# Gathering the experts' tokens in plain float32, two experts at a time, with two more weight blocks in the ring

## The chip, the cores and the metric

The kernel runs on one core of a Trainium2 chip. TensorE multiplies matrices into PSUM (eight banks of 128 x 512 float32 here); VectorE, ScalarE and GpSimd work on SBUF, and the first two also read PSUM; SyncE (SP) issues nearly all DMA transfers that bring weights from HBM. The metric is the device time of one execution in microseconds; a kernel's time is the median of several runs.

## What is computed

The program is two transformer blocks one after the other on 256 tokens of width 1024. The first is a token mixer (attention, gated linear attention, a long convolution), followed by a mixture of experts; the second has two layers, each with attention, a convolutional feed-forward part and a gated projection. Only the mixture of experts, near the middle, is touched. It adds to the residual stream `x`:

```
h = modulate(rms_norm(x, norm2_g), shift2, scale2)
x = x + gate2[:, None, :] * grouped_moe(h, router_w, router_b,
                                        moe_w_gate, moe_w_up, moe_w_down)
```

For every token the router scores 16 experts in 4 groups, keeps the best group and in it the best two experts, and weights them. An expert e computes `(silu(h Wg[e]) * (h Wu[e])) Wd[e]` with Wg and Wu of 1024 x 512 and Wd of 512 x 1024, in float32.

## The kernel before

All instructions are unrolled and their order on each engine is the order in which the Python code emits them (`manual_schedule`). Every operation on TensorE, ScalarE and VectorE goes through the helper `Clocked` (line 379 in the profile's rows), so the rows are told apart by the names of their tiles.

**Precision.** A weight that is used with full precision elsewhere is split into two rounded halves of the type float32r (`T2`, `split`, `mm3`), and three products of halves replace one. Experts use plain float32 matmuls (type F32 on both sides). The gather before the change multiplies both float32r halves of the tokens, `h2H` and `h2L`, by a selection matrix.

**Router.** `ev_out` receives the output projection, forms `x1`, and per half of 128 tokens the normed tokens `h` (`h2s[m]`). `normed2` finishes them. `high(m)` rounds them on ScalarE into `h2H`, `low(m, n)` forms the rest `h2L` on VectorE (for the second half, m = 1, on GpSimd, lines 1591 and 1592). Scores, the two best and their ranks follow on VectorE in instructions of at most 128 x 128 elements (`scores`, `sel`, `ge`, `gt`, `cnt`, `top`, `gs`, `cg`, `mask`); one group of matmuls against `mask` counts, per expert, the tokens ahead. `rank` gives each token its slot in each expert, of 64.

**A branch.** If an expert has more than 64 tokens, a slow body runs (line 1696). It is not taken here, but all engines read the flag from memory and branch. One `gather` ahead of it has its `dp` formed before the branch and its matmuls after it.

**Gather.** `gather(q)` is a Python generator that serves four experts. It forms `dp` (tokens x 4 experts x 64 slots, ones and zeros), then for two quarters of the width multiplies `h2H` and `h2L` (stationary, 128 x 128) by `dp` (moving, 256 columns), 32 matmuls in all, and copies the results into two tiles `xg`. `way(g)` turns `dp` of two experts round (`back`, to send results home) and gathers their gates (`gsl`). A generator runs in steps: at `side.tick()` the planner `Side` runs the next step if the modelled TensorE clock `Clocked.now["P"]` has passed the step's due time, which is the modelled end of what the previous step gave VectorE or ScalarE. For TensorE the model charges columns / 2400 us, four times that for plain float32.

**Experts.** The loop at line 1855 takes one expert after the other. `gate_up(e, i, ps)` uses one 1 MB block of weights: the 64 gathered tokens are stationary, the weights move (512 columns), gate and up in the two column halves of the array. `hidden` turns the result round and forms `hid`; `down(g)` multiplies a pair of experts by the down weights; its result `y` is scaled and split into two halves, and `combine(g - 1)` adds the pair into four PSUM banks `pa` that stay for the whole stage. That leaves four banks for everything else. `gather(1)` is added at expert 1, the next at experts 5 and 9.

**Weights.** The DMA ring holds whole blocks of 1 MB in SBUF slots of 8 KB per partition (`u8`, 19 slots); `load(depth)` issues transfers until `depth` blocks are there or under way, and SP waits in order for each slot. During the experts the depth is `RAW_MOE + 2` = 17; with `h2H` and `h2L` these are the 19 slots. One more block, the 18th, is loaded at line 1627 in two halves into two 4 KB slots (`u4`, 8 slots, which also hold `gate2`, `xg`, `h` and the split `y`).

Of the kernel before, what the change touches and what calls it, by code (L numbers as in the profile page):

```python
# [9 lines left out]
F32 = mybir.dt.float32  # L10
F32R = mybir.dt.float32r
# [7 lines left out]
D = 1024  # L19
# [305 lines left out]
BUFS = {"u8": 19, "u4": 8, "u2": 6, "u1": 4, "uh": 4, "us": 7}  # L325
LAST = 8
RAW = {None: 3, "last": 2, "mod1": 8, "moe_gu": 9, "moe_down": 9}
RAW_MOE = 15
STEPS2 = (1, 1, 1, 0)
STEPS1 = (1, 2, 2, 0, 0, 1, 0, 2)  # L330
PIECES = {"k": 2, "c": 2, "3": 3, "": 1}
# [88 lines left out]
def program(ctx, tc, A, out, dump=None):  # L420
# [80 lines left out]
    def load(depth=None):  # L501
        at = order[pieces[min(pos["take"], len(pieces) - 1)][0]]
        at = "last" if at[0][:8] == "ffn_down" and at[1] >= LAST else at[0]
        while pos["raw"] < len(order):
            i = pos["raw"]
            name, b, kt, cols, _ = order[i]
            if len(raws) >= (depth or (RAW_MOE + 2 if at[:3] == name[:3] == "moe" else RAW.get(at, RAW[None]))):
                break
            if len(raws) >= RAW_MOE + 2:
                raws[i] = [T([128, cols], "raw", tag="u4") for _ in range(kt)]  # L510
                for k, t in enumerate(raws[i]):
                    nc.sync.dma_start(t, A[name][b][:, k * cols:k * cols + cols])
            else:
                t = T([128, kt, cols], "raw", tag="u8")
                nc.sync.dma_start(t.rearrange("p k c -> p (k c)"), A[name][b])
                raws[i] = t if name[:3] != "moe" else [t[:, k] for k in range(kt)]
            pos["raw"] += 1
# [988 lines left out]

    x1 = T([128, 2, D], "x1")

    h2s, rs, h2, turned = {}, {}, [], []

    def ev_out(m, n, ps):

        gate1, shift2, scale2, _ = mod2
        if m and not n:
            turned.extend(turned_half(h2s[0][0], k4) for k4 in range(2))
        c = slice(n * 512, n * 512 + 512)
        if n == 0:
            h2s[m] = T([128, D], "h2"), T([128, 2], "ss2")
        h, ss = h2s[m]
        V.tensor_tensor(x1[:, m, c], ps, gate1[:, c], op=OP.mult)  # L1520
        V.tensor_tensor(x1[:, m, c], x1[:, m, c], xt[:, m, c], op=OP.add)
        j = T([128, 512], "junk2")
        S.activation(j, x1[:, m, c], AF.Square, accum_out=ss[:, n:n + 1])
        V.tensor_tensor(h[:, c], x1[:, m, c], scale2[:, c], op=OP.mult)
        if m and n:
            load(RAW_MOE)
        if not n:
            if m:
                normed2(0)
            return  # L1530
        V.tensor_tensor(ss[:, 0:1], ss[:, 0:1], ss[:, 1:2], op=OP.add)
        rs[m] = rsqrt1(ss[:, 0:1], 1e-6, D)

    def normed2(m, ns=(0, 1)):

        if not m:
            h2.extend(T2([128, 2, D], "h2"))
        h = h2s[m][0] if 0 in ns else h2s[m]
        h2s[m] = h
        for n in ns:  # L1540
            c = slice(n * 512, n * 512 + 512)
            V.scalar_tensor_tensor(h[:, c], h[:, c], rs[m], mod2[1][:, c], op0=OP.mult, op1=OP.add)

    def high(m):
        S.activation(h2[0][:, m], h2s[m], AF.Copy)

    def low(m, n, eng=V):
        c = slice(n * 512, n * 512 + 512)
        eng.tensor_tensor(h2[1][:, m, c], h2s[m][:, c], h2[0][:, m, c], op=OP.subtract)

    pa = [{}, {}]

# [10 lines left out]
    for k4 in range(2):  # L1563
        turned.append(turned_half(h2s[1][0], k4))
        if not k4:
            logits(turned, psr[:, 0:16], True, False)
            residual(0)
    high(0)
    logits(turned[2:], psr[:, 16:32], False, True)
    normed2(1, (0,))  # L1570
    for i in range(1, 3):
        residual(i)
    low(0, 0)
    h2H, h2L = h2
    gate2 = mod2[3]
    dump("x1", x1)

# [8 lines left out]
        V.scalar_tensor_tensor(sg[:, m], psr[:, m * 16:m * 16 + 16], rs[m], st["shifted"], op0=OP.mult, op1=OP.add)  # L1586
    S.activation(sg, sg, AF.Tanh, scale=0.5)
    normed2(1, (1,))
    high(1)
    for n in range(2):  # L1590
        low(1, n, G)
    sel = R(E3, "sel")
    V.scalar_tensor_tensor(sel, sg, 0.5, rb.unsqueeze(1).to_broadcast(E3), op0=OP.mult, op1=OP.add)

    def ahead(v, count):
# [19 lines left out]
    mask = R(E3, "mask")  # L1615
    V.scalar_tensor_tensor(mask.rearrange("p m (g e) -> p (m g) e", e=4), cg2.unsqueeze(2).to_broadcast([128, 8, 4]), 0.5, cnt,
                           op0=OP.is_lt, op1=OP.mult)
    low(0, 1)

    ps = PS()  # L1620
    mf = mask.rearrange("p m e -> p (m e)")
# [14 lines left out]

    grouped = {}

    def gather(q):

        dp = dps[q] = T([128, 2, 4, 64], "dp", F32R)
        shape = [128, 2, 4, 64]
        V.tensor_tensor(dp, rank[:, :, 4 * q:4 * q + 4].unsqueeze(3).to_broadcast(shape),
                        C("slots").unsqueeze(1).unsqueeze(1).to_broadcast(shape), op=OP.is_equal)
        yield
        xg = xgs[q] = [T([128, 4, 4, 64], "xg") for _ in range(2)]
        for k4 in range(2):
            banks = [PS(), PS()]
            for w, src in enumerate((h2H, h2L)):
                for k2, ps in enumerate(banks):  # L1650
                    for m in range(2):
                        for k in range(2):
                            c = slice((k4 * 4 + 2 * k2 + k) * 128, (k4 * 4 + 2 * k2 + k) * 128 + 128)
                            P.matmul(ps[:, k * 256:k * 256 + 256], src[:, m, c], dp[:, m].rearrange("p a s -> p (a s)"),
                                     start=w + m + k == 0, stop=w + m + k == 3)
                if w == 0 and q:
                    yield
            for k2, ps in enumerate(banks):
                p4 = ps.rearrange("p (k a s) -> p k a s", k=2, a=4)
                if k2:  # L1660
                    V.tensor_copy(xg[k4][:, 2:4], p4)
                else:
                    S.activation(xg[k4][:, 0:2], p4, AF.Copy)
            yield

    def way(g):

        d = dps[g // 2][:, :, g % 2 * 2:g % 2 * 2 + 2].rearrange("p m a s -> p m (a s)").bitcast(F32)
        ps = PS()
        for m in range(2):  # L1670
            P.transpose(ps[:, m * 128:m * 128 + 128], d[:, m], ident)
        for a in range(2):
            for m in range(2):
                P.matmul(ps[a * 64:a * 64 + 64, 256:257], d[:, m, a * 64:a * 64 + 64], kept[:, m, 2 * g + a:2 * g + a + 1], start=m == 0, stop=m == 1)
        back, gsl = T([128, 256], "back", F32R), T([128, 1], "gsl")
        S.activation(back, ps[:, :256], AF.Copy)
        V.tensor_copy(gsl, ps[:, 256:257])
        grouped[g] = (back, gsl)

    xgs, dps = {}, {}  # L1680
    first = gather(0)
    next(first)

# [75 lines left out]
    def gate_up(e, i, ps):  # L1759

        w = take("moe_gu", 4 * e + i)
        for k in range(2):
            x = xgs[e // 4][i // 2][:, (2 * i + k) % 4, e % 4]
            for a, q in enumerate((low, high)):
                P.matmul(ps[q], x, w[k][:, a * 512:a * 512 + 512], start=i + k == 0, stop=i + k == 4)
        if i == 3:
            t = T([128, 512], "gu")
            S.activation(t, ps, AF.Copy)
            gated[e] = t
# [13 lines left out]
    def down(g):  # L1783


        back, gsl = grouped.pop(g)
        hid = hids.pop(g)
        ps = [PS(), PS()]
        last = g == N_EXP // 2 - 1
        done[g] = back, []  # L1790
        for i in range(2):
            if not (last and i):
                ws = [take("moe_down", 4 * g + 2 * a + i) for a in range(2)]
            for k, n in ((k, n) for n in range(2) for k in range(2)) if last and i else ((k, n) for k in range(2) for n in range(2)):
                if last and i and not k:
                    wn = take("moe_down", 4 * g + 1 + 2 * n)
                for a, q in enumerate((low, high)):
                    w = wn[a][:, k * 512:k * 512 + 512] if last and i else ws[a][k][:, n * 512:n * 512 + 512]
                    P.matmul(ps[n][q], hid[:, a, 2 * i + k], w, start=i + k == 0, stop=i + k == 2)
                if i and k:  # L1800
                    y = T([128, 512], "y")
                    V.scalar_tensor_tensor(y, ps[n], gsl, gate2[:, n * 512:n * 512 + 512], op0=OP.mult, op1=OP.mult)
                    if not last:
                        hl = T2([128, 512], "y")
                        split(*hl, y)
                    done[g][1].append(y if last else hl)
# [47 lines left out]

    for e in range(N_EXP):
        g = e // 2
        if e % 4 == 1 and e + 3 < N_EXP:
            nxt = side.add(gather(e // 4 + 1))
        ps = PS()
        for i in range(4):  # L1860
            gate_up(e, i, ps)
            if i == 1 and e:
                hidden(e - 1)
            if i == 0 and e % 2:
                way(g)
            if i == 2 and e % 2 and g:
                combine(g - 1)
            if i != 1:
                side.tick()
        if e % 4 == 3 and e + 1 < N_EXP:  # L1870
            side.finish(nxt)
        if e % 2 == 0 and g:
            down(g - 1)
# [490 lines left out]
```

## Time and profile before

| what | value |
|---|---|
| median of 3 runs | 1422.9 us (1419.89 to 1423.99) |
| the profiled execution's own time | 1417.77 us |
| its span from first to last instruction | 1416.0 us |
| mean granted TensorE clock over the span | 0.994 |
| busy: TensorE matmul, weight load, VectorE, ScalarE | 96%, 75%, 59%, 45% |
| weights and other data read from HBM | 295 MB |

The times of the profile are microseconds from the first instruction. PE is TensorE's matmul, PEld its weight load, DVE is VectorE, ACT ScalarE, POOL GpSimd. A row names the tile written, an arrow, and the tiles read, buffer numbers left out. Because matmuls overlap, the ends of matmul rows are modelled; the distance from one start to the next is the better measure of what a group costs. The clock of TensorE is given as a share of 2.4 GHz; 0.50 is its other level, 1.2 GHz.

### The profile page before, as it was taken

What the parts mean: (1) busy time and instruction counts of PE and PEld (TensorE: products, weight loads), DVE (VectorE), ACT (ScalarE), POOL (GpSimd) and SP (SyncE); (2) the same over time, 40 slices, a digit from 0 to 9 for tenths busy, and PEclk for the clock granted to TensorE, in tenths of its full rate; (3) what the DMA queues carried; (4) which work ended last, traced back from release to release, by engine and by line L of the source; (5) the groups of instructions that cost most, each with busy time, mean ns of one, the idle gap of its engine ahead of it and who ended that gap; (6) DMA issues with size and microseconds to landing.
All of it is one profiled execution on the core that took longest, in us unless ns stands there. A gap on an engine that the chain in (4) does not pass through costs nothing.

```text
span 1416.0 us, 20480 instructions
## 1 busy us (share of the span) xinstructions
PE 1365.2 (96%) x8334; PEld 1064.8 (75%) x8334; DVE 836.7 (59%) x1517; ACT 635.8 (45%) x1021; POOL 8.3 (1%) x15
## 2 busy tenths in 40 slices
PE   5999999999999899999999899999999998999998
PEld 2678899878797444343488679999978887999996
DVE  4777457445866511211475586666676888566675
ACT  4643465534433311111356555445536664455541
POOL 0000000000000000000000000000000000000000
PEclk9999999999999999999999999999999999999999
DMA  9523334635469799999742345655544354555630
GB/s 370 223 71 119 149 150 153 250 125 190 175 212 360 301 421 421 421 421 421 283 179 90 120 149 181 207 179 208 175 156 146 127 179 139 188 179 180 216 140 30
DMA packets 44482, 297.42 MB, mean 210 GB/s; under 512 B 5171, under 2 KB 6371, under 8 KB 10017
## 3 DMA queue, kind: packets, MB, share of 16 engines
q1 hardware_dynamic: 41868, 291.02, 54.6%
q10 hardware_dynamic: 1924, 3.27, 0.7%
q0 software_dynamic: 592, 1.79, 0.5%
q8 instruction: 67, 1.10, 0.3%
q14 instruction: 31, 0.25, 0.0%
HBM read 295.00 MB, written 1.05 MB: 209 GB/s over the span
## 4 chain that ended last, share of the span: by engine, by line
PE 58%; DVE 5%; ACT 2%; issue 1%; DVEq 0%; ACTq 0%
PE ps L379 48%; PE pd L379 7%; DVE w L379 1%; PE pa L379 1%; PE pq L379 1%; ACT pe L379 1%; DVE v L379 1%; PE oc L379 1%; DVE sm L379 1%; DVE rs L379 0%; ACT w L379 0%; DVE xL L379 0%; DVE rsa L379 0%; ACT xH L379 0%; ACT oc L379 0%
## 5 line engine op out<-in xcount | busy, mean ns | idle before, releaser
L379 DVE TENSOR_TENSOR w<-raw,w 128x1024 fp32r<-128x1024 f32 (+3 forms) x301 | 346.5, 1195 | 84.6 <-ACT w L379 83.5
L379 ACT ACTIVATE w<-raw 128x1024 fp32r<-128x1024 f32 (+3 forms) x301 | 293.5, 1033 | 10.8 <-DVE w L379 4.8
L379 PE MATMUL ps<-xH,w 128*128 128x256 f32 x1408 | 256.5, 283 | 0.6 <-ACT xH L379 0.6
L379 PEld LDWEIGHTS ps<-xH,w 128*128 128x128 f32 x1408 | 220.6, 192 | 1.8 <-ACT xH L379 1.1
L379 PE MATMUL ps<-xL,w 128*128 128x256 f32 x704 | 199.4, 283 | 0.7 <-DVE xL L379 0.7
L379 PE MATMUL ps<-w,xH 128*128 128x512 f32 (+2 forms) x544 | 150.3, 362 | 4.0 <-ACT xH L379 2.1
L379 PEld LDWEIGHTS ps<-xL,w 128*128 128x128 f32 x704 | 135.0, 192 | 1.8 <-DVE xL L379 1.1
L379 PE MATMUL pd<-w,fh 128*128 128x512 f32 x528 | 125.6, 395 | 0.0
L379 PE MATMUL ps<-raw,xg 128*64 128x512 f32 x512 | 120.0, 600 | 0.0
L379 PE MATMUL ps<-hH,w 128*128 128x256 f32 (+1 forms) x608 | 115.7, 287 | 0.0
L379 PEld LDWEIGHTS pd<-w,fh 128*128 128x128 f32 x528 | 98.2, 189 | 21.6
L379 PEld LDWEIGHTS ps<-w,xH 128*128 128x128 f32 x544 | 95.4, 189 | 19.3 <-ACT xH L379 4.0
L379 PEld LDWEIGHTS ps<-hH,w 128*128 128x128 f32 (+1 forms) x608 | 94.9, 187 | 7.9 <-issue 2.7
L379 PE MATMUL ps<-w,xL 128*128 128x512 f32 (+2 forms) x272 | 97.8, 360 | 1.9 <-DVE xL L379 1.7
L379 PE MATMUL ps<-w,hH 128*128 128x512 f32 (+1 forms) x288 | 88.1, 390 | 0.0
L379 PE MATMUL ps<-hL,w 128*128 128x256 f32 (+1 forms) x304 | 85.9, 283 | 0.0
L379 PEld LDWEIGHTS ps<-raw,xg 128*64 128x64 f32 x512 | 33.3, 137 | 55.7 <-issue 51.9
L379 DVE SCALAR_TENSOR_TENSOR fc<-ps,par,fc 128x255 f32<-128x255 f32 x88 | 42.4, 482 | 51.5 <-ACT fc L379 49.9
L379 ACT ACTIVATE fc<-ps,par 128x256 f32<-128x256 f32 x44 | 24.8, 564 | 92.3 <-PE ps L379 66.4
L379 PEld LDWEIGHTS ps<-w,hH 128*128 128x128 f32 x288 | 52.2, 188 | 13.8 <-issue 2.7
L379 PEld LDWEIGHTS ps<-w,xL 128*128 128x128 f32 x272 | 51.3, 189 | 11.9 <-DVE xL L379 5.1
L379 PE MATMUL ps<-raw,hid 128*64 128x512 f32 x256 | 57.4, 593 | 0.0
(445 smaller groups left out, 1858.7 us busy)
## 6 DMA issues: line engine op xcount, KB each, us to landing
raw<-in_moe_gu SPq DMA_DIRECT2D x63, 1024.0 KB, 14.1
raw<-in_moe_down SPq DMA_DIRECT2D x32, 1024.0 KB, 12.8
raw<-in_mod SPq DMA_DIRECT2D x24, 1024.0 KB, 5.0
raw<-in_ffn_gate SPq DMA_DIRECT2D x22, 1024.0 KB, 4.8
raw<-in_ffn_up SPq DMA_DIRECT2D x22, 1024.0 KB, 4.9
raw<-in_ffn_down SPq DMA_DIRECT2D x22, 1024.0 KB, 4.8
raw<-in_w_brg SPq DMA_DIRECT2D x12, 1024.0 KB, 5.9
raw<-in_ple_gate SPq DMA_DIRECT2D x8, 1024.0 KB, 4.8
```

What stands on the lines that cost most here:

```text
L379: return f(*args, **kw)
```

## The change

The rounded halves `h2H` and `h2L` go, with `high`, `low` and their instructions on ScalarE, VectorE and GpSimd. `gather(g)` now serves two experts: `dp` and `h` are plain float32, a gather is 16 matmuls of 128 columns, and what `way` did is the generator's last step. The gather of the next pair is added at every even expert. The rest of the first gather runs after the second block of expert 0. The two 8 KB slots that the halves held go to the ring: the depth during the experts becomes 19, and line 1627 loads up to 20 blocks; the load in `ev_out` still stops at 15.

```diff
-RAW_MOE = 15
+RAW_MOE = 17
...
         if m and n:
-            load(RAW_MOE)
+            load(RAW_MOE - 2)
...
-        if not m:
-            h2.extend(T2([128, 2, D], "h2"))
...
-    def high(m):
-        S.activation(h2[0][:, m], h2s[m], AF.Copy)
-
-    def low(m, n, eng=V):
-        c = slice(n * 512, n * 512 + 512)
-        eng.tensor_tensor(h2[1][:, m, c], h2s[m][:, c], h2[0][:, m, c], op=OP.subtract)
...
-    high(0)
...
-    low(0, 0)
-    h2H, h2L = h2
...
     normed2(1, (1,))
-    high(1)
-    for n in range(2):
-        low(1, n, G)
...
-    low(0, 1)
...
-    def gather(q):
-
-        dp = dps[q] = T([128, 2, 4, 64], "dp", F32R)
-        shape = [128, 2, 4, 64]
-        V.tensor_tensor(dp, rank[:, :, 4 * q:4 * q + 4].unsqueeze(3).to_broadcast(shape),
+    def gather(g):
+
+        dp = T([128, 2, 2, 64], "dp")
+        shape = [128, 2, 2, 64]
+        V.tensor_tensor(dp, rank[:, :, 2 * g:2 * g + 2].unsqueeze(3).to_broadcast(shape),
                         C("slots").unsqueeze(1).unsqueeze(1).to_broadcast(shape), op=OP.is_equal)
+        d = dp.rearrange("p m a s -> p m (a s)")
         yield
-        xg = xgs[q] = [T([128, 4, 4, 64], "xg") for _ in range(2)]
+        xg = T([128, 8, 2, 64], "xg")
+        grouped[g] = xg,
         for k4 in range(2):
-            banks = [PS(), PS()]
-            for w, src in enumerate((h2H, h2L)):
-                for k2, ps in enumerate(banks):
-                    for m in range(2):
-                        for k in range(2):
-                            c = slice((k4 * 4 + 2 * k2 + k) * 128, (k4 * 4 + 2 * k2 + k) * 128 + 128)
-                            P.matmul(ps[:, k * 256:k * 256 + 256], src[:, m, c], dp[:, m].rearrange("p a s -> p (a s)"),
-                                     start=w + m + k == 0, stop=w + m + k == 3)
-                if w == 0 and q:
-                    yield
...
+            ps = PS()
+            for m in range(2):
+                for k in range(4):
+                    c = slice((k4 * 4 + k) * 128, (k4 * 4 + k) * 128 + 128)
+                    P.matmul(ps[:, k * 128:k * 128 + 128], h2s[m][:, c], d[:, m], start=m + k == 0, stop=m + k == 4)
+            p4 = ps.rearrange("p (k a s) -> p k a s", k=4, a=2)
+            if k4:
+                V.tensor_copy(xg[:, 4:], p4)
+            else:
+                S.activation(xg[:, :4], p4, AF.Copy)
             yield
-
-    def way(g):
-
-        d = dps[g // 2][:, :, g % 2 * 2:g % 2 * 2 + 2].rearrange("p m a s -> p m (a s)").bitcast(F32)
...
-            x = xgs[e // 4][i // 2][:, (2 * i + k) % 4, e % 4]
+            x = grouped[e // 2][0][:, 2 * i + k, e % 2]
...
-        if e % 4 == 1 and e + 3 < N_EXP:
-            nxt = side.add(gather(e // 4 + 1))
+        if e % 2 == 0 and e + 2 < N_EXP:
+            nxt = side.add(gather(g + 1))
...
-            if i == 0 and e % 2:
-                way(g)
+            if e == 0 and i == 1:
+                for _ in first:
+                    pass
...
-        if e % 4 == 3 and e + 1 < N_EXP:
+        if e % 2 and e + 1 < N_EXP:
             side.finish(nxt)
```

## Rows read from the trace of the kernel before

**Rows 1.** Busy time by stretch: length, busy time and count per engine, clock, DMA share, GB/s.
```profile
500.00:685.00 185.00, 185.00 (x923) 73.09 (x921) 30.62 (x56) 26.83 (x53) 0.00 (x0) 1.00 1.01 420
```

**Rows 2.** Chain of waits, 523 to 578 us: start, length, what.
```profile
523.44 22.98 PE ps L379 x114
546.42 2.06 PE pa L379 x8
548.49 27.83 PE ps L379 x146
```

**Rows 3.** Waits of weight loads, 478 to 690 us: total, times, longest.
```profile
PEld ps L379 <- issue: 107.6, 335, 0.8
...
PEld ps L379 <- DMA raw<-in_moe_gu: 0.7, 3, 0.3
```

**Rows 4.** Groups of TensorE instructions by form: busy us, mean ns, idle before.
```profile
L379 PE MATMUL ps<-dp,h2H 128*128 128x256 f32 x64 | 10.3, 308 | 0.3 <-PEq L1696 0.3
...
L379 PE MATMUL oc<-vc,pp 128*128 128x128 f32 x64 | 8.2, 283 | 0.0
```

**Rows 5.** Timeline around one old gather group: start, length, engine, what, count.
```profile
493.28 1.02 PEld L379 LDWEIGHTS ps<-dp,h2H 128*128 128x128 f32 x8 [0.81 <-issue]
493.28 1.22 PE L379 MATMUL ps<-dp,h2H 128*128 128x256 f32 x8
...
494.43 0.20 PEld L379 LDWEIGHTS ps<-raw,xg 128*64 128x64 f32 x4
```

**Rows 6.** Timeline of weight loads at two groups in plain float32.
```profile
1144.22 1.87 PEld L379 LDWEIGHTS oc<-vc,pp 128*128 128x128 f32 x16
1146.01 0.30 PEld L379 LDWEIGHTS ps<-w,xH 128*128 128x128 f32 x2
...
784.15 1.87 PEld L379 LDWEIGHTS ps<-diag,pe 128*128 128x128 f32 x16
786.13 0.73 PEld L379 LDWEIGHTS ps<-qkT 64*128 64x128 f32 x8
```

**Rows 7.** Timeline of the router on TensorE, VectorE and GpSimd.
```profile
462.47 1.97 PE L379 MATMUL ps<-par,h2T 128*128 128x16 f32 x16
...
464.30 0.69 DVE L379 TENSOR_TENSOR h2L<-h,h2H 128x512 fp32r<-128x512 f32 x1
464.91 0.37 DVE L379 SCALAR_TENSOR_TENSOR scores<-ps,rs,shifted 128x16 f32<-128x16 f32 x2
...
465.86 0.19 DVE L379 SCALAR_TENSOR_TENSOR sel<-scores,rb 128x32 f32<-128x32 f32 x1
...
467.12 2.48 POOL L1549 TENSOR_TENSOR h2L<-h,h2H 128x512 fp32r<-128x512 f32 x2 [54.04 <-ACT h2H L379]
467.27 1.15 DVE L379 SCALAR_TENSOR_TENSOR top<-cnt,sel 128x32 f32<-128x32 f32 x1
...
468.67 0.97 DVE L379 TENSOR_TENSOR ge<-gs 128x32 f32<-128x32 f32 x1
```

**Rows 8.** Timeline of TensorE from the mask to the first expert.
```profile
470.66 1.86 PE L379 MATMUL ps<-mask,c_base 128*128 128x32 f32 x8 [4.40 <-DVE mask L379]
...
474.71 2.05 PE L379 MATMUL ps<-dp,h2H 128*128 128x256 f32 x8 [0.30 <-PEq L1696]
...
479.62 8.80 PE L379 MATMUL ps<-raw,xg 128*64 128x512 f32 x40
```

**Rows 9.** Busy time and clock in three short stretches with or behind a pause.
```profile
470.00:472.00 2.00, 1.34 (x7) 1.37 (x7) 1.07 (x4) 0.00 (x0) 0.00 (x0) 0.50 0.17 70
801.00:802.00 1.00, 0.00 (x0) 0.00 (x0) 0.07 (x1) 0.90 (x5) 0.00 (x0) 1.00 0.03 8
1163.00:1164.00 1.00, 1.00 (x4) 0.81 (x4) 0.75 (x1) 0.88 (x2) 0.00 (x0) 0.50 1.00 426
```

**Rows 10.** Timeline of VectorE: the last instruction of its list at expert 0.
```profile
488.83 0.15 DVE L379 TENSOR_SCALAR lam<-par 128x1 f32<-128x1 f32 x1
```

**Rows 11.** Timeline of ScalarE: the second half of the first split `y`.
```profile
518.10 0.63 ACT L379 ACTIVATE y<-y 128x512 fp32r<-128x512 f32 x1 [2.77 <-PE ps L379]
```

More of the change, by code (lines that the diff above doesn't have):

```diff
@@ L1507, in program @@
     x1 = T([128, 2, D], "x1")
-    h2s, rs, h2, turned = {}, {}, [], []
+    h2s, rs, turned = {}, {}, []
     def ev_out(m, n, ps):
@@ L1637, in program @@
     grouped = {}
-    def gather(q):
-        dp = dps[q] = T([128, 2, 4, 64], "dp", F32R)
-        shape = [128, 2, 4, 64]
-        V.tensor_tensor(dp, rank[:, :, 4 * q:4 * q + 4].unsqueeze(3).to_broadcast(shape),
+    def gather(g):
+        dp = T([128, 2, 2, 64], "dp")
+        shape = [128, 2, 2, 64]
+        V.tensor_tensor(dp, rank[:, :, 2 * g:2 * g + 2].unsqueeze(3).to_broadcast(shape),
                         C("slots").unsqueeze(1).unsqueeze(1).to_broadcast(shape), op=OP.is_equal)
+        d = dp.rearrange("p m a s -> p m (a s)")
         yield
-        xg = xgs[q] = [T([128, 4, 4, 64], "xg") for _ in range(2)]
+        xg = T([128, 8, 2, 64], "xg")
+        grouped[g] = xg,
         for k4 in range(2):
-            banks = [PS(), PS()]
-            for w, src in enumerate((h2H, h2L)):
-                for k2, ps in enumerate(banks):
-                    for m in range(2):
-                        for k in range(2):
-                            c = slice((k4 * 4 + 2 * k2 + k) * 128, (k4 * 4 + 2 * k2 + k) * 128 + 128)
-                            P.matmul(ps[:, k * 256:k * 256 + 256], src[:, m, c], dp[:, m].rearrange("p a s -> p (a s)"),
-                                     start=w + m + k == 0, stop=w + m + k == 3)
-                if w == 0 and q:
-                    yield
[L1658 to L1663, printed above, removed]
+            ps = PS()
[8 more added lines that the diff above has]
+                S.activation(xg[:, :4], p4, AF.Copy)
             yield
-    def way(g):
-        d = dps[g // 2][:, :, g % 2 * 2:g % 2 * 2 + 2].rearrange("p m a s -> p m (a s)").bitcast(F32)
         ps = PS()
@@ L1677, in way @@
         V.tensor_copy(gsl, ps[:, 256:257])
-        grouped[g] = (back, gsl)
-    xgs, dps = {}, {}
+        grouped[g] = (xg, back, gsl)
     first = gather(0)
@@ L1783, in down @@
     def down(g):
-        back, gsl = grouped.pop(g)
+        _, back, gsl = grouped.pop(g)
         hid = hids.pop(g)
```

## The prediction, made before the changed kernel was run

> **What bounds the kernel now.** I began with the busy times by stretch. Between 500 and 685 us, where the experts run, two things look full at once: TensorE is busy in the whole 185 us, and the DMA engines show a share of 1.01 at 420 GB/s [rows 1]. Only one of them can set the pace, so the next view is the chain of waits: there a pair of experts costs TensorE either 22.98 us or 27.83 us beside 2.06 us of combining, and DMA is in no step of it [rows 2]. The two kinds alternate, because one gather serves four experts and its matmuls fall into every second pair; the gather therefore costs 27.83 - 22.98 = 4.85 us per four experts, paid in full. The waits of the weight loads agree: 107.6 us in 335 pieces of at most 0.8 us are "issue", the engine held by its own earlier matmuls, and for expert weights it waited 0.7 us in three pieces [rows 3]. So TensorE bounds the stage and the weights keep ahead of it. A block of 1.049 MB at 420 GB/s takes 2.50 us, while TensorE uses 24 blocks in 54.94 us (the two kinds of pair with their combines), 2.29 us each: DMA is the slower, but it begins with 18 blocks in hand and the 78 others cost only 78 x 0.21 = 16 us of that lead, some seven blocks.
>
> **The gathers in the loop.** This is the large term. Before, the gather of four experts is 32 matmuls of 256 columns on rounded halves; the record has 64 for one half (there are as many for the other), 128 for four gathers, one instruction each [rows 4]. Eight of them take 1.15 us from their first weight load to the next one of the experts [rows 5]; by the chain, a group costs 4.85 / 4 = 1.21, so each insertion adds about 0.06 beside its own time. The new gather has 16 matmuls of 128 columns per two experts, with plain float32 on both sides. A plain float32 matmul is two instructions: those into `oc` are 32 in the code (four calls of 2 x 2 x 2, line 2185) and 64 in the trace [rows 4]. The new kind is already there elsewhere: `oc` and `diag` multiply a 128x128 float32 block by 128 float32 columns. Sixteen of their instructions take 1.79 us in one place and 1.98 in another [rows 6]. I take the middle, 1.88, plus 0.06 for the insertion: 1.94 for a group of eight matmuls. A pair needs two groups, 3.9 us; seven gathers run in the loop, so 14 x 1.94 = 27.15 us stand where three gathers of 4.85, 14.55 us, stood: +12.6 us, with bounds of 14 x 1.85 and 14 x 2.04, which is +11.35 and +14.0. Nothing hides it, since these matmuls use all 128 columns of an engine that has no pause. The number of evacuations to `xg`, of `dp` elements and of `back` transposes per expert stays as it is, on engines that wait for TensorE.
>
> The Trainium skill ("TensorE: Matmul & The Clock Gate", LDWEIGHTS) has a load of 128 columns at about 107 ns. By that alone a group could not take less than 16 x 107 ns = 1.71 us, and the term would be 14 x 1.77 - 14.55 = +10.2 us, an estimate from that page; the rows above are slower, and I go by them.
>
> **The router before the loop.** VectorE forms `low(0, 0)` in 0.69 us just ahead of the scores. The scores also need the router matmuls, which end at 462.47 + 1.97 = 464.44; they start at 464.91 and could start at about 464.50: -0.4 us. `high` on ScalarE was never waited for there, and `low(0, 1)` comes after the mask: both at nothing. The larger part is GpSimd's `low(1)`. While it runs, from 467.12 for 2.48 us, two VectorE instructions on 128x32 elements take 1.15 us (`top`) and 0.97 us (`ge`), and `sel`, of the same size ahead of it, takes 0.19 [rows 7]. By starts that is 0.96 us for the first and, with `gt` able to follow `ge` as soon as it does elsewhere, about 0.68 for the second: -1.64. Together -2.05 us, between -1.6 and -2.2.
>
> The Trainium skill ("GPSIMD Engine Reference", its table of the engine's figures) says that GpSimd shares its SBUF interfaces with VectorE and contends with instructions that have two SBUF inputs. The trace agrees: both stretched instructions have two.
>
> **The first gather.** It lies wholly on the path, from 474.71 to the first expert matmul at 479.62, 4.91 us [rows 8]. The new one is 16 matmuls, 32 instructions at 1.88 / 16 = 0.1175: 3.76 us. The TensorE clock was granted at 0.50, its 1.2 GHz level, after the router's pause [rows 9], and the first eight matmuls took 2.05 us there against 1.22 later [rows 5, 8]. If that stays, the new one loses the same 0.8 and saves 0.35. If the shorter pause (466.25 to about 468.6, 2.3 us) leaves the clock up, 0.8 more is saved there and about 0.9 in the mask matmuls, which took 1.86 us [rows 8]. Other pauses tell both: in a microsecond without a matmul at 801 it stands at 1.00, and at 1163, after another pause, at 0.50 [rows 9]. Since the pause for the branch follows at once, I take the low level: -0.35, bounds -2.05 and +0.2.
>
> **New waits.** (a) Gather 1 is now added at expert 0, and VectorE works off a long list there (`rot`, `lam`) that ends 9.36 us after the first expert matmul, at 488.98 [rows 8, 10]; then come `gsl` and `dp` of pair 1. When TensorE is sent to gather is decided by the planner's clocks. By its own prices (four times columns / 2400 for float32, so 3.41 us per block) VectorE stands 10.8 us ahead of TensorE when the loop starts, so the third block of expert 0, at 10.7 with the transposes of `back`, is just too early; `dp` is issued after the fourth and the matmuls after the first block of expert 1. On the chip five blocks are the 40 instructions that took 8.80 us with their drain [rows 8]; with some 0.6 for `back` that is 9.3 us after the start, while `dp` is there at about 10.1: TensorE waits, with all expert matmuls queued behind it, +0.8 us, once. Bounds: 0, and 2.6 if the gather comes one block sooner. (b) The 4 KB slots. Before, pair 0's second half of `y` was split 2.77 us late, at 518.10, when a TensorE matmul had given a slot back; ScalarE waited, TensorE did not [rows 11]. Now the two `h` tiles stay until the last gather, and the block loaded in halves is the 20th, used at expert 3's last step, after `combine(0)`. By count at the end of expert 2: `gate2`, two `h`, two `xg`, two half blocks are 7 of 8, and `down(0)` asks for two. The second comes free inside `combine(0)`, and TensorE then waits for ScalarE's 0.63 us [rows 11], VectorE's 0.69 for as many elements [rows 7] and two handovers: +1.5 us, once; lower bound 0, if a slot is free after all. What VectorE and ScalarE have queued behind that (`gsl`, `hid` of expert 2) is wanted only by `down(1)`, a whole expert later.
>
> **Two more weight blocks.** Two loads that stood behind the release of `x1` can go out at about 461 us, in a gap of the DMA engines. TensorE waits for no weights, so this is worth between 0 and -0.7 us; I take 0. Later stages get the same loads at the same place of the list: 0, give or take 1.
>
> **Sum.** 12.6 - 2.05 - 0.35 + 0.8 + 1.5 = +12.5 us. The profiled execution took 1417.8 us (a span of 1416.0), so it would become 1430.3; it lies 5.1 below the median of the three runs, 1422.9, and by that the median becomes 1435.4. All low ends: 11.35 - 2.2 - 2.05 - 0.7 = +6.4, 1429.3. All high ends: 14.0 - 1.6 + 0.2 + 2.6 + 1.5 = +16.7, 1439.6.
>
> **Rivals.** First, the other side: *weights set the pace*. For it: DMA share 1.01, and TensorE's loads are busy only 73.09 of 185 us, 40% [rows 1]. Then the gather slides into pauses and each block in hand is worth 2.50 us: 1422.9 - 5.0 = 1417.9. It decides from the point at which TensorE waits for weights at all. Against it: those waits are 0.7 us, and a pair with gather is longer by exactly the gather [rows 2, 3]. The Trainium skill ("Perfetto Trace Analysis", Identifying the Most-Contended Engine) judges TensorE's headroom by its weight loads' busy share and not by matmul busy time, which gives this rival its case; the chain speaks against it. 5%. Second, *half the matmuls*: were a 128-column float32 matmul one instruction, a group would cost 0.94 + 0.06, the term would be 14.0 - 14.55, and the total -0.65: 1422.3. The 64 records of `oc` for 32 calls exclude it nearly [rows 4]; 3%. Third, *a mild loss*: the clock stays up and neither new wait comes, 12.6 - 2.05 - 2.05 = +8.5: 1431.4; 22%. Fourth, *the waits come back in every pair*: 0.8 us at each of the six later gathers, +4.8: 1440.2; 12%. Against it, from gather 2 on the planner issues `dp` two expert blocks, 3.4 us, ahead of the matmuls that read it. My forecast keeps 58%.
>
> **How the numbers follow.** 1428 to 1441 takes in the bounds, cut by a little at the low end where all gains would have to meet, and the third and fourth cases, which leaves out about one in ten. About 0.3% (4.3 us) is what a measurement of this kernel tells from no change. Faster by more: the first rival, 0.05. Within it: the second, and the rim of the third, 0.06. Slower: 0.89.
>
> **What would show it.** A pair of experts in the chain: about 22.98 + 3.9 = 26.9 us in every pair from the second on, none at 22.98 but the last. Matmuls that read `h` and `dp`: 256, in groups of 16 within 1.8 to 2.0 us. `top` and `ge` near 0.2 us, and no GpSimd instruction there. The first expert matmul near 477.2 us. DMA share in the stage below 1.00, as the ring fills. One wait of TensorE for `dp` and one for a split `y`, near experts 1 and 3. The prediction is wrong if the groups take clearly less than 1.7 us, if waits for weights vanish that I did not see, or if a new wait returns in each pair.

## The result

The changed kernel takes 1439.4 us in the median (1439.29 to 1444.19) where the kernel before takes 1422.2: a ratio of 1.0118 with a 95% interval of 1.0087 to 1.0149, some 17 us slower. The prediction was slower, 1435.4 within 1428 to 1441. The profiled execution of the changed kernel took 1439.29 us, with a span of 1437.5.

The chain of waits of the changed kernel answers to [rows 2]: start, length, what.

```profile
473.51 5.86 PE ps L379 x32
...
489.34 38.05 PE ps L379 x216
527.39 1.15 PE pa L379 x4
...
528.61 0.64 ACT y L379
529.27 0.70 DVE y L379
...
530.01 0.97 PE pa L379 x3
530.98 27.25 PE ps L379 x146
558.23 2.06 PE pa L379 x8
560.29 27.25 PE ps L379 x146
...
677.54 22.23 PE ps L379 x104
```

Every pair but the last now costs 27.25 us: there are five such pieces, and none at 22.98 between them. A pair's gather is 27.25 - 22.98 = 4.27 us, where 4.85 us served two pairs before. `combine(0)` stands in two parts, with ScalarE and VectorE between them; of that below.

The loop as a whole is read from the first matmul of the experts to the start of the last combine. This is the timeline of TensorE, the kernel before in the first fence (its first expert matmul is in [rows 8]) and the changed kernel in the second.

```profile
694.65 0.70 PE L379 MATMUL pa<-y,back 128*128 128x512 f32 x1
```

```profile
479.29 3.65 PE L379 MATMUL ps<-raw,xg 128*64 128x512 f32 x16
...
713.10 1.13 PE L379 MATMUL pa<-y,back 128*128 128x512 f32 x2
```

Before it is 694.65 - 479.62 = 215.03 us, after it is 713.10 - 479.29 = 233.81: +18.8. In what follows "the loop" is this distance. The spans differ by 21.5; what is left over lies outside the loop, and "The sum" below takes it up.

The waits of the weight loads in the changed kernel, 478 to 705 us, stand against [rows 3]: total, times, longest. Behind the "..." is its stretch from 500 to 685 us, against [rows 1].

```profile
PEld ps L379 <- issue: 106.1, 325, 3.1
...
PEld ps L379 <- DMA raw<-in_moe_gu: 0.6, 2, 0.3
...
500.00:685.00 185.00, 184.01 (x968) 79.51 (x968) 28.90 (x56) 25.79 (x51) 0.00 (x0) 1.00 0.99 409
```

TensorE is still the engine that is full, and for gate and up weights it waited 0.6 us in two pieces, as little as before. The two more blocks had nothing to shorten.

### The profile page after: what moved, and what is told of

Same layout as the page of the kernel before. It is cut to its first block, busy times and chain, and to the rows that moved or that the text cites. A ratio compares the mean times of both kernels' runs of the same rounds, so it can differ in the third digit from the quotient of the medians.

```text
span 1437.5 us, 20727 instructions
## 1 busy us (share of the span) xinstructions
PE 1386.3 (96%) x8462; PEld 1082.6 (75%) x8462; DVE 834.2 (58%) x1519; ACT 633.7 (44%) x1019; POOL 5.8 (0%) x13
## 3 DMA queue, kind: packets, MB, share of 16 engines
q0 software_dynamic: 592, 1.79, 0.4%
## 4 chain that ended last, share of the span: by engine, by line
PE 57%; DVE 6%; ACT 3%; issue 1%; DVEq 0%; ACTq 0%
PE ps L379 48%; PE pd L379 7%; DVE w L379 2%; PE pa L379 1%; PE pq L379 1%; ACT pe L379 1%; DVE v L379 1%; DVE sm L379 1%; ACT w L379 0%; DVE rs L379 0%; PE oc L379 0%; DVE xL L379 0%; DVE rsa L379 0%; ACT xH L379 0%; DVE bs L379 0%
## 6 DMA issues: line engine op xcount, KB each, us to landing
raw<-in_moe_down SPq DMA_DIRECT2D x32, 1024.0 KB, 10.8
```

## The experiments

### What a gather costs: precision, grouping, or where it is put

The change does two things to the gather at once. Each was made alone. First the precision: plain float32, still four experts at once. Shown is the matmul; with it `high` and `low` go, and the ring has 19 blocks.

```diff
-                 P.matmul(ps[:, k * 256:k * 256 + 256], src[:, m, c], dp[:, m].rearrange("p a s -> p (a s)"),
-                          start=w + m + k == 0, stop=w + m + k == 3)
+                 P.matmul(ps[:, k * 256:k * 256 + 256], h2s[m][:, c], dp[:, m].rearrange("p a s -> p (a s)"),
+                          start=m + k == 0, stop=m + k == 2)
```

> The kernel before with one part of the change alone, the precision: plain float32 tokens and dp, but still four experts at once, with the old schedule; no halves, no high and low; the freed slots go to the ring (19 blocks), no half block. Nothing is left out. A gather has 32 instructions of 256 columns. Theory (the columns set the price of plain float32: the last combine's 8 plain instructions of 512 columns take 3.63 us, 0.454 each, so 256 columns take 0.227): 7.3 us per four experts in the chain in place of 4.85, a pair with gather at about 30.2 us, loop +7.4, with the first gather about +3 and the router about -2: 8 to 9 us slower than the kernel before. Rival (the weight loads set the price, 32 loads at 0.117 us as in the changed kernel's groups): 3.8 to 4.0 us per four experts, pairs with gather at 27.0, 4 to 6 us faster than the kernel before.

Its chain of waits:

```profile
532.63 22.98 PE ps L379 x114
...
557.67 30.93 PE ps L379 x146
```

A gather of four experts costs 30.93 - 22.98 = 7.95 us: the columns set the price, as the first theory had it, a little above its 7.3. The loop is 224.28 us, +9.25, which is three times 7.95 - 4.85. The time is 1.007 (1.0042 to 1.0097) of the kernel before, 10 us where 8 to 9 were expected.

Then the grouping: rounded halves as before, two experts at once.

```diff
-        dp = dps[q] = T([128, 2, 4, 64], "dp", F32R)
+        dp = T([128, 2, 2, 64], "dp", F32R)
...
+                P.matmul(ps[:, k * 128:k * 128 + 128], src[:, m, c], d[:, m], start=w + m + k == 0, stop=w + m + k == 5)
...
-        if e % 4 == 1 and e + 3 < N_EXP:
-            nxt = side.add(gather(e // 4 + 1))
+        if e % 2 == 0 and e + 2 < N_EXP:
+            nxt = side.add(gather(g + 1))
```

> The kernel before with the other part alone, the grouping: two experts at once, with the changed kernel's schedule of gathers, on the rounded halves (high and low stay, ring of 17 blocks). Nothing is left out. A gather of a pair has 32 instructions of 128 columns in float32r. Theory (at 128 columns the weight loads set the price, about 0.11 to 0.12 us each, whatever the type): 3.6 to 4.3 us per pair, pairs at 26.6 to 27.3 us, loop +11 to +15, wait for dp as in the changed kernel, 12 to 16 us slower than the kernel before, as much as plain float32. Rival (columns set the price: half of the old group): 2.45 us per pair, pairs at 25.4, loop +2.6, 3 to 5 us slower than the kernel before.

Its chain of waits:

```profile
533.60 27.15 PE ps L379 x146
```

A pair costs 27.15 - 22.98 = 4.17 us, all but the 4.27 of plain float32. So with two experts at once the type hardly matters, and the grouping alone brings nearly the whole loss of the gathers, 7 x 4.17 - 3 x 4.85 = +14.6 us. The two parts don't add: per four experts the gather costs 4.85 us before, 7.95 with the precision alone, 8.34 with the grouping alone, 8.54 with both. The loop is 231.95 us, +16.9. The expected wait for `dp` isn't in it: in this run the clock is still low when the experts begin, their first two blocks take 6.27 us and not 3.65 as in the changed kernel, and `dp` is there in time. The time is 1.0131 (1.0091 to 1.0172) of the kernel before, 18.6 us where 12 to 16 were expected; 2.6 of it is this low clock in the profiled execution.

Two runs separate a gather's own instructions from the cost of putting them between the experts' matmuls. In one, both groups of the new gather follow one another (on top of `no_waits`, below):

```diff
-            yield
+            if k4 or not g:
+                yield
```

> The kernel no_waits with one edit: in the loop both groups of a gather (16 instructions each) follow one another, in place of one block of an expert between them. Nothing is left out. Theory (a group costs 1.98 us by its own instructions and 0.15 us for being put between the experts' matmuls, 2.13 together): one insertion less per pair, pairs in the chain at 27.10, seven times 0.15 = 1.05 us faster than no_waits. Rival (the 0.15 is part of each group's own time): pairs at 27.25, the same time as no_waits.

In the other, the kernel before does without one of its pauses in a gather:

```diff
-                if w == 0 and q:
-                    yield
```

> The kernel before with one edit: in the loop the two halves of a gather's quarter follow one another, so that a gather of four experts is put between the experts' matmuls twice and not four times. Nothing is left out. Theory (to put a group between the experts' matmuls costs 0.35 us beside its own instructions, as one_go showed: pairs at 26.90 for 27.25): a pair with gather at 27.83 - 2 x 0.35 = 27.13 us, three times, 2.1 us faster than the kernel before. Rival (the 0.06 us per insertion that the prediction worked with): pairs with gather at 27.71, 0.4 us faster.

The chains of waits, the first run (with its weight loads of one gather) and then the second:

```profile
525.98 26.90 PE ps L379 x146
...
533.66 3.65 PEld L379 LDWEIGHTS ps<-dp,h 128*128 128x128 f32 x32 [0.81 <-issue]
```

```profile
525.24 22.98 PE ps L379 x114
...
550.28 27.15 PE ps L379 x146
```

One insertion less saves 27.25 - 26.90 = 0.35 us in the first; two less save 27.83 - 27.15 = 0.68 in the second, 0.34 each. The first run beat its expectation (0.15), the second met it to 0.02 us. So an insertion costs about 0.35 us, not 0.06. The weight loads agree without the chain: 32 in one go take 3.65 us, 16 take 1.86 in the changed kernel (shown further below), so the second 16 add 1.79. The whole loop of the first run is 2.12 us shorter than that of `no_waits`, where seven times 0.35 would be 2.45; why the rest is missing isn't shown. Its time is 1.0064 (1.0037 to 1.0092) of the kernel before.

With the insertions taken off, at this price in all four kernels, what is left is the instructions' own price:

| gather | us in the chain | insertions | instructions | us of one instruction |
|---|---|---|---|---|
| halves, four experts (before) | 4.85 | 4 | 32 of 256 columns | (4.85 - 1.36) / 32 = 0.109 |
| halves, two experts | 4.17 | 2 | 32 of 128 columns | (4.17 - 0.70) / 32 = 0.108 |
| plain, four experts | 7.95 | 4 | 32 of 256 columns | (7.95 - 1.36) / 32 = 0.206 |
| plain, two experts (the change) | 4.27 | 2 | 32 of 128 columns | (4.27 - 0.70) / 32 = 0.112 |

At 128 columns an instruction costs 0.108 to 0.112 us in either type, and on halves 256 columns cost no more. The Trainium skill ("TensorE: Matmul & The Clock Gate", LDWEIGHTS) gives the load of P columns as P / 1.2 ns, by which 128 columns take about 107 ns, an estimate from that page; the three rows of the table near 0.11 agree with it. The second row tells the load from the columns: half the columns of the first row, at the same price, so there the load of the 128x128 stationary block is most likely the bound. In plain float32 256 columns cost 0.206; there the columns are the limit. In the other two rows columns and load come to about the same, and the runs don't tell them apart: half of 0.206 is 0.103 for 128 plain columns, and the combine's eight matmuls of 512 columns on halves take 2.06 us, (2.06 - 0.35) / 8 = 0.214 each, so 256 columns would take 0.107 (estimates). So the change pays as many instructions for half the experts as before, and by either measure none of them is cheaper. `fewer_steps` is 0.9977 (0.9965 to 0.9989) of the kernel before in time, 3.3 us; its loop is 212.93 us, -2.1.

### What the freed space is worth

The ring of the changed kernel was set back to 17 blocks, and then to 5, without the half block in both; the comparison is `no_half` (next part), which has 19.

```diff
-RAW_MOE = 17
+RAW_MOE = 15
...
-            load(RAW_MOE - 2)
+            load(RAW_MOE)
...
-    load(RAW_MOE + 2 + 1)
+    load(RAW_MOE + 2)
```

> The changed kernel with a ring of 17 weight blocks as before (the two freed 8 KB slots stay empty) and no half block, so it differs from no_half by the two slots alone. Nothing is left out. Theory (TensorE sets the pace and waits 1.1 us for weights in the whole stage, so two more blocks are worth nothing): within 0.7 us of no_half, waits for weights of the experts under 2 us, pairs at 27.25 us. Rival (weights set the pace, each block in hand is worth 2.50 us): 5.0 us slower than no_half, with as much waiting for moe_gu and moe_down blocks.

```diff
-RAW_MOE = 17
+RAW_MOE = 3
...
-            if len(raws) >= RAW_MOE + 2:
+            if len(raws) >= 19:
...
-    load(RAW_MOE + 2 + 1)
+    load(RAW_MOE + 2)
```

> The changed kernel with a ring of 5 blocks during the experts, no half block. Nothing is left out. Theory (with the new gathers TensorE uses 12 blocks in 29.3 us, 2.44 us each, and DMA brings one in 2.50 us, so that even a short ring only has to cover (2.50 - 2.44) x 91 = 5.5 us of lag): between 0 and 8 us slower than no_half, pairs in the chain at 27.3 to 28.3 us. Rival (each block in hand is worth 2.50 us): 14 blocks fewer, 35 us slower than no_half.

With 17 blocks the loop is 232.29 us, to the digit what it is with 19. With 5 it is 233.89; this is 1.6 us more, and the busy times of the run with 5 by stretch tell where from: length, busy time per engine, clock, DMA share, GB/s.

```profile
488.00:492.00 4.00, 4.00 (x19) 3.06 (x19) 0.00 (x0) 1.03 (x2) 0.00 (x0) 0.57 1.01 422
500.00:685.00 185.00, 185.00 (x972) 80.06 (x972) 28.97 (x56) 25.92 (x51) 0.00 (x0) 1.00 1.01 421
```

The granted clock was at 0.57 in the mean behind the wait for `dp`, which costs (1 - 0.57) x 4 = 1.7 us and happens to lie inside the loop here (in `no_half` the clock stood at 1.00 there; its first gather, ahead of the loop, was the one at the low clock, and took 6.28 us against 4.33 with 5 blocks). Its pairs cost 27.25 us like those of the changed kernel, and its table of waits has none of an expert's matmuls for DMA. The medians agree: 1437.9 us with 17, 1436.1 with 5, 1436.5 with 19. Fourteen blocks less cost nothing that can be measured. With 5 blocks the DMA engines are full (1.01 at 421 GB/s) and just keep pace. The rival of the prediction in which weights set the pace falls by both runs: it would have had 5 and 35 us more.

### The two new waits

`no_half` leaves out the block in two halves; `no_waits` moves, on top of that, the gather of the second pair from expert 0 to expert 1.

```diff
-    load(RAW_MOE + 2 + 1)
+    load(RAW_MOE + 2)
```

> The changed kernel with one edit: the block that is loaded in two halves into two 4 KB slots is not loaded early; the ring stays at 19 blocks. Nothing is left out of the computation. Theory (the pause of TensorE inside combine(0), 1.45 us between its two groups of matmuls into pa, comes from the 4 KB slots that the two half blocks hold): the pause falls under 0.2 us, the pairs in the chain stay at 27.25 us, the wait for dp stays at 2.2 us, and the span is 1.45 us shorter than the changed kernel's, where the clock falls at the same places. Rival (the pause comes from ScalarE's and VectorE's own order, not from slots): the pause stays at 1.45 us and the time is the same.

```diff
-        if e % 2 == 0 and e + 2 < N_EXP:
+        if (e == 1 if g == 0 else e % 2 == 0) and e + 2 < N_EXP:
```

> The kernel no_half with one more edit: the gather of the second pair is added at expert 1 and not at expert 0; later pairs as in the changed kernel. Nothing is left out. Theory (the wait of 2.2 us for dp is due to the gather being sent too early behind VectorE's list at expert 0): both waits are gone, the span is 3.65 us shorter than the changed kernel's in all, and the remaining distance of the loop to the kernel before is the gathers' matmuls alone, 7 x 4.27 - 3 x 4.85 = +15.3 us. Rival (the wait moves on to the next gather, because it is VectorE's queue as such that is late): a wait of 1 to 2 us for dp shows up at expert 1 or 2 and the gain is 1.45 us only.

The first combine in the chain of `no_half`, then that of `no_waits` from the first gather on:

```profile
527.56 2.06 PE pa L379 x8
529.62 27.25 PE ps L379 x146
```

```profile
472.99 51.94 PE ps L379 x290
524.93 2.06 PE pa L379 x8
```

In `no_half` the combine is in one piece of 2.06 us again; the loop is 232.29 us, 1.52 shorter. In `no_waits` TensorE doesn't wait for `dp` at all, and the loop is 229.74, 2.55 shorter once more. Both waits are what they were taken for, and neither moves on to another place. What remains is 229.74 - 215.03 = +14.7 us of gathers; 7 x 4.27 - 3 x 4.85 = 15.3 had been expected. The times are 1.0099 (1.007 to 1.0129) and 1.0072 (1.0049 to 1.0095) of the kernel before, so without its waits the change still loses 10 us.

### The router and the clock

On the kernel before, the halves stay, but none of `low` runs on GpSimd or ahead of the scores:

```diff
-    low(0, 0)
...
-    for n in range(2):
-        low(1, n, G)
...
     next(first)
+    for m, n in ((0, 0), (1, 0), (1, 1)):
+        low(m, n)
```

> The kernel before with the rounding moved alone: the differences h2L are formed on VectorE after dp of the first gather (the first one still in time for the gather's second half), none on GpSimd and none ahead of the scores. Nothing is left out. Theory (the router loses 1.64 us to GpSimd's two instructions and 0.4 to the difference ahead of the scores): top and ge at 0.19 us, the mask 2.05 us sooner after the transposes of h, and the whole kernel about 2 us faster if the differences, now 4 x 0.69 us on VectorE behind dp, come in time for the gather's matmuls on h2L; up to 1 us of it goes where they don't. Rival (the two slow instructions are due to their operands or to DMA traffic, not to GpSimd): top and ge stay near 1 us and the gain is 0.4.

VectorE and TensorE of this run (against [rows 7, 8]):

```profile
468.32 0.19 DVE L379 SCALAR_TENSOR_TENSOR top<-cnt,sel 128x32 f32<-128x32 f32 x1
...
468.77 0.19 DVE L379 TENSOR_TENSOR ge<-gs 128x32 f32<-128x32 f32 x1
```

```profile
469.97 1.68 PE L379 MATMUL ps<-mask,c_base 128*128 128x32 f32 x8 [2.23 <-DVE mask L379]
...
474.88 2.05 PE L379 MATMUL ps<-dp,h2H 128*128 128x256 f32 x8 [1.34 <-DVEq L1695]
476.73 1.91 PE L379 MATMUL ps<-dp,h2L 128*128 128x256 f32 x8
478.43 1.91 PE L379 MATMUL ps<-dp,h2H 128*128 128x256 f32 x8
...
481.31 8.80 PE L379 MATMUL ps<-raw,xg 128*64 128x512 f32 x40
```

`top` and `ge` take 0.19 us each where they took 1.15 and 0.97, so it was GpSimd. The Trainium skill ("GPSIMD Engine Reference", its table of the engine's figures) has it that GpSimd contends for SBUF with VectorE's instructions of two SBUF inputs; the pair of runs agrees. The mask comes 2.17 us sooner, counted from the transposes of `h` (before at 458.95, here at 460.43). But none of it reaches the experts in this execution. Behind the branch TensorE waits 1.3 us for VectorE's queue, until the three `low` behind `dp` are worked off (they end at 474.68), and the granted clock is 0.50 from 474 to 478 us, so that three of the gather's four groups run at the low level. The first expert matmul comes 481.31 - 460.43 = 20.88 us after the transposes of `h`, before it was 479.62 - 458.95 = 20.67. The time is 0.9974 (0.9958 to 0.9991) of the kernel before all the same, 3.7 us by the ratio, where about 2 were expected; the profile doesn't show where that lies. The profiled execution of the kernel before, 1417.77 us, is shorter than each of the timed ones (1417.87 at the least), so others of them may lose more here; this isn't shown.

On top of `router`, `router_warm` adds matmuls in TensorE's pauses, for the clock alone:

```diff
+    warm = PS("warm")
+    for _ in range(3):
+        nc.tensor.matmul(warm, ident, x1[:, 0, :512], start=True, stop=True)
...
     residual(3)
+    nc.tensor.matmul(warm, ident, x1[:, 0, :512], start=True, stop=True)
```

> The kernel router with four plain float32 matmuls of 512 columns added on TensorE, three in the router's pause and one after the counting matmuls; their result goes to a bank that is not read. Nothing is left out. Theory (the clock is at 1.2 GHz in the mask and first gather because TensorE has nothing to do for 2.3 to 4.4 us ahead of them): granted clock 1.00 from 470 to 477, mask matmuls at about 1.0 us (1.15 to 1.86 now) and the first eight gather matmuls at 1.2 (2.05), 1.5 to 2 us faster than router. Rival (the clock falls for another reason, or the added work delays the mask): the same time as router or up to 1 us slower.

TensorE and the stretch from 470 to 478 us:

```profile
467.68 2.74 PE L1575 MATMUL warm<-x,c_base 128*128 128x512 f32 x6
470.26 0.96 PE L379 MATMUL ps<-mask,c_base 128*128 128x32 f32 x8
...
474.45 1.18 PE L379 MATMUL ps<-dp,h2H 128*128 128x256 f32 x8 [1.42 <-DVEq L1699]
...
470.00:474.00 4.00, 3.03 (x13) 1.64 (x12) 3.21 (x8) 1.24 (x1) 0.00 (x0) 1.00 0.44 182
474.00:478.00 4.00, 3.55 (x30) 3.58 (x31) 0.94 (x2) 0.64 (x2) 0.00 (x0) 1.00 0.92 285
```

The clock stays at 1.00 through both pauses; the mask matmuls take 0.96 us (1.86 in [rows 8]), the first group of the gather 1.18 (2.05). The first expert matmul comes 17.90 us after the transposes of `h`, where it was 20.88 in `router` and 20.67 before. The time is 0.997 (0.9953 to 0.9987) of the kernel before; the median, 1420.75 us, is no better than that of `router` (1421.06). So the 3.0 us between the two profiles, where 1.5 to 2 were expected, don't show in the times.

### Better than both kernels

`fewer_steps` and `router_warm` together, and:

```diff
-    low(0, 1)
+    low(0, 0)
+    low(1, 0)
...
-    for m, n in ((0, 0), (1, 0), (1, 1)):
-        low(m, n)
+    low(0, 1)
+    low(1, 1)
```

> What the runs point to, on the kernel before: fewer_steps and router_warm together, with two of the four differences h2L on VectorE while TensorE counts the mask and two behind dp. Nothing is left out; the four added matmuls go to a bank that is not read. Theory: the parts add up, 2.1 us from the insertions, 2.8 from the router and the clock, 0.7 more since VectorE is done with h2L sooner: 5 to 6 us faster than the kernel before. Rival (the parts take from one another, or the differences beside the counting hold up rank and dp): no better than router_warm, 3 us.

From the transposes of `h` to the last combine this kernel takes 230.25 us, before it is 694.65 - 458.95 = 235.70: -5.45, the sum of the parts. The time is 0.9977 (0.9962 to 0.9991) of the kernel before, 3.3 us by the ratio where 5 to 6 were expected: better than both kernels, and no more than `fewer_steps` alone. Behind the experts its profiled execution takes 4.8 us longer than that of the kernel before, in these stretches:

```profile
723.00:727.00 4.00, 3.61 (x9) 2.85 (x10) 2.35 (x7) 0.60 (x1) 0.00 (x0) 0.58 0.54 221
788.00:792.00 4.00, 4.00 (x19) 3.82 (x20) 1.69 (x10) 1.89 (x6) 0.00 (x0) 0.57 0.00 0
802.00:806.00 4.00, 3.65 (x18) 3.56 (x20) 2.06 (x11) 0.65 (x2) 0.00 (x0) 0.57 0.00 0
```

Here the clock fell three times, 1.7 us each by (1 - 0.57) x 4, where that of the kernel before stood at 1.00 in its profile. Whether a stage that ends sooner makes such falls more frequent, or they fall by chance, stays open: over all timed executions the mean granted clock of this kernel is 0.991, that of the kernel before 0.990, which is no sign of more falls and too coarse to exclude them.

## Why the prediction was right, and where its sizes were off

**TensorE as the bound: right.** The pairs, the waits for weights and the runs with 17 and 5 blocks agree.

**The gathers in the loop: right in kind, 2.7 us too small.** The term was +12.6 and is 7 x 4.27 - 14.55 = +15.3, above its upper bound of 14.0. The weight loads of two groups in the changed kernel and of the experts' matmuls behind them, against [rows 5]:

```profile
489.31 1.86 PEld L379 LDWEIGHTS ps<-dp,h 128*128 128x128 f32 x16 [3.06 <-issue]
491.29 0.20 PEld L379 LDWEIGHTS ps<-raw,xg 128*64 128x64 f32 x4
...
493.15 1.86 PEld L379 LDWEIGHTS ps<-dp,h 128*128 128x128 f32 x16 [0.81 <-issue]
495.14 0.20 PEld L379 LDWEIGHTS ps<-raw,xg 128*64 128x64 f32 x4
```

From load to load a group takes 1.98 us, the upper of the two rows of [rows 6], and in the chain 4.27 / 2 = 2.13. The step that failed is the insertion at 0.06 us. It was got as 1.21 - 1.15 from a distance [rows 5] that already holds most of the insertion, so it was counted as the group's own time. By the runs, a group's instructions take (4.27 - 0.70) / 2 = 1.79 us, the lower row of [rows 6], and each insertion 0.35: 14 x 2.13. The prediction's estimate by the Trainium skill ("TensorE: Matmul & The Clock Gate", LDWEIGHTS), 1.71 us for a group, was nearer to these 1.79 than the 1.88 that it went by. The insertion is wrong there in the same way.

**The router: right.** -2.05 was predicted; the mask comes 2.16 us sooner, counted from the transposes of `h` (460.62 in the changed kernel). VectorE and TensorE of the changed kernel:

```profile
468.51 0.19 DVE L379 SCALAR_TENSOR_TENSOR top<-cnt,sel 128x32 f32<-128x32 f32 x1
...
470.17 1.15 PE L379 MATMUL ps<-mask,c_base 128*128 128x32 f32 x8 [2.24 <-DVE mask L379]
...
473.51 5.84 PE L379 MATMUL ps<-dp,h 128*128 128x128 f32 x32 [0.30 <-PEq L1671]
479.29 3.65 PE L379 MATMUL ps<-raw,xg 128*64 128x512 f32 x16
```

**The first gather: wrong in sign, and covered.** It was to save 0.35 us, with 0.2 more as the upper bound, and costs 5.78 - 4.91 = 0.87 more. The low clock was foreseen, but its loss was taken over as the 0.8 us of the old first group. Here the level held for most of the gather: from 476 to 478 us the granted clock is 0.56, before it was 0.81. The mask matmuls, most of them ahead of the fall this time, gave 0.71 back (1.86 to 1.15). Up to the first expert matmul the sum is -2.0 where -2.4 was predicted.

**Wait for `dp`: 2.2 us, not 0.8.** The planner's margin was worked out as 10.8 us against 10.7 and went the other way: TensorE was sent to the gather after expert 0's fourth block, one block sooner. The bound for that case, 2.6, held:

```profile
489.34 2.02 PE L379 MATMUL ps<-dp,h 128*128 128x128 f32 x16 [2.20 <-DVE dp L379]
```

A margin of 0.1 us out of 10.8 decides nothing; the likelier value should have lain between the cases. That it doesn't come back in later pairs was right, since the five pairs are equal.

**Wait for the split `y`: right.** +1.5 was predicted; between the two parts of the combine lie 530.01 - 527.39 - 1.15 = 1.47 us, with ScalarE and VectorE in the order foreseen, and `no_half` takes them away by the slots alone.

**Two more blocks: right**, at nothing. The DMA share in the stage fell to 0.99, as foreseen.

**The sum.** In the loop 15.3 + 2.2 + 1.5 = 19.0 against 18.8 measured; with -2.0 ahead of it +16.8 for the change, where the medians show +17.2. The spans differ by 4.7 us more than that, 1.7 before the router and 3.0 behind the experts, and this is the clock at other places. Busy times by stretch, the kernel before first; 789 and 803 in it are the places of 808 and 822 in the changed kernel:

```profile
368.00:372.00 4.00, 3.65 (x20) 3.17 (x21) 2.35 (x5) 0.19 (x1) 0.00 (x0) 1.00 0.00 0
789.00:793.00 4.00, 2.81 (x21) 2.74 (x22) 2.83 (x14) 3.10 (x10) 0.00 (x0) 1.00 0.01 4
803.00:807.00 4.00, 4.00 (x34) 3.35 (x35) 2.04 (x10) 1.58 (x3) 0.00 (x0) 1.00 0.02 4
```

```profile
368.00:372.00 4.00, 3.58 (x9) 2.81 (x10) 1.66 (x3) 0.26 (x1) 0.00 (x0) 0.57 0.00 0
808.00:812.00 4.00, 3.30 (x16) 3.33 (x17) 2.38 (x13) 2.01 (x8) 0.00 (x0) 0.61 0.00 2
822.00:826.00 4.00, 2.95 (x14) 2.98 (x15) 2.65 (x13) 0.65 (x2) 0.00 (x0) 0.57 0.00 0
```

At 0.57 a stretch of 4 us loses 1.7. At 368 us both kernels run the same code, and of the kernels built on the old one `router_warm` and `fewer_steps` show the same fall there; so the one at 368 isn't the change's. The two behind the experts don't come with the new gathers as such: `no_waits`, which has the same gathers, shows none between 480 and 1180 us. That they fell here by chance isn't shown.

**The number.** That 1439.4 lies inside 1428 to 1441 is in part luck. The change of +16.8 is as much as the sum of all high ends, +16.7: the gathers and the first gather went beyond their upper bounds, and both waits came near theirs. The range was wide enough because it took in the fourth rival, whose 1440.2 is nearer to the measured time than the forecast's own 1435.4; but the wait that it has in every pair came once.

## What to carry to other kernels

A gather by matmul costs at least by the stationary blocks that it loads: fill the moving side until its columns take as long as the load, here about 256 columns of rounded halves or 128 of plain float32, and compare types only at equal filling. Price an insertion into a stream of other matmuls from the chain, by a run with one less; a distance to the next load hides part of it. Before memory is freed for more prefetch, look whether the engine waits for it at all: here a ring of 5 did what a ring of 19 does.

## What the runs showed of the hardware that had not been expected

A float32r matmul instruction of 128 columns is no cheaper than one of 256 (0.108 and 0.109 us), and a plain float32 instruction of 128 costs nearly the same (0.112). Each insertion of a gather's group into the full stream of the experts' matmuls cost 0.34 to 0.35 us beside the group's own instructions; what it consists of the runs don't tell. Four matmuls whose result nobody reads, put into pauses, kept the granted clock at 1.00 and made the mask matmuls twice as fast (0.96 for 1.86 us) in both kernels that have them.
